# Second products of a feed-forward layer: 16 of 22 chunks of the sum by 2 x 2 blocks in three layers of four, with sums of weights made by adding transfers

## The chip, the cores and the metric

The kernel runs on one core of one Trainium2 chip. The metric is the device time of one execution in microseconds (us). Before the change the median of three runs is 2431.68 us (2431.58 to 2431.84).

## What is computed

Two layers of a transformer are applied to 512 rows of 1024 numbers, all in 32-bit floats. Each layer has a feed-forward network (FFN), a mix of three kinds of attention, and a second FFN, each with a residual sum and a layer norm. So there are four FFNs in a run. The part that the change touches is the product with `w2`:

```python
D_MODEL, SEQ, DEPTH, D_FF = 1024, 512, 2, 2816

def _swiglu(x, w1, w2):
    gt, up = jnp.split(x @ w1, 2, axis=-1)
    return (jax.nn.silu(gt) * up) @ w2

def reference(x, ...):
    for l in range(DEPTH):
        x = _layer_norm(DN_ALPHA * x + 0.5 * _swiglu(x, ffn1_w1[l], ffn1_w2[l]), ln1_g[l], ln1_b[l])
        mix = _token_mix(x, ...)
        x = _layer_norm(DN_ALPHA * x + mix, ln2_g[l], ln2_b[l])
        x = _layer_norm(DN_ALPHA * x + 0.5 * _swiglu(x, ffn2_w1[l], ffn2_w2[l]), ln3_g[l], ln3_b[l])
    return x
```

Here h = silu(gt) * up has 512 rows and 2816 columns, and `w2` has 2816 rows and 1024 columns.

## The kernel before

**Precision.** A 32-bit operand x is split into a high part (`hi`, ScalarE copies x to the matmul's format) and a rest (`lo`, VectorE subtracts the high part from x). A product of two operands is three matmuls: hi by hi, rest by hi, hi by rest. `wsplit` (lines 155 to 162) makes the two parts of a chunk of weights: one ScalarE instruction at line 160 and one VectorE instruction at line 161, 1024 elements in each partition.

**The second product.** The sum over 2816 runs in 22 chunks (`KF`) of 128. The result, 512 x 1024, lies in eight banks of PSUM, `accs[tb][hf]`: four blocks of rows by two halves of columns. A plain chunk costs 4 x 2 x 3 = 24 matmuls of 128x512 (`mm_rows`, line 195).

**Blocks.** `short_rows` (line 410) takes 12 chunks together as a 2 x 2 block product: the 512 rows in two halves, the 12 chunks in two halves of `NW` = 6, the 1024 columns in two halves. With seven products of blocks in place of eight (a Strassen-like scheme) it needs sums of parts of h and sums of blocks of weights first, and adds results into several quarters of the output afterwards. The quarters are `c11`, `c12`, `c21`, `c22`, two banks each; the blocks of h are `a11` to `a22`. One *step* of a product takes one pair of chunks of weights: `prod`, 2 banks x 2 chunks x 3 = 12 matmuls of 128x512 (line 453). Seven products of three steps are 21 steps. In the names that the change introduces the products are E, P, Z, S, T, R and F; in the code before they are `f_e`, `f_1`, `f_z`, `f_6`, `f_7`, `f_r` and `f_4`. E, P, S, T and F write into `c21`, Z into `c12`, R into `c11`. After E, P, S and T, `copies` takes `c21` to SBUF on ScalarE (line 459) and `add` adds the copy into another quarter on VectorE (line 464), which reads and writes that quarter's bank in PSUM.

**What runs around it.** Four plain chunks, 12 to 15 (`LEAD`), run ahead of the steps, while the first six transfers of weights into the tiles `b1` and `bt` land. Behind the steps follow chunk 16 and 17, plain, and then the last four, 18 to 21, in an order by rows, so that the layer norm can begin on the first 128 rows (`rows_ln`). The old input `xa` of the layer norm is loaded back from DRAM by POOL's queue into the space that `short_rows` leaves (line 622).

**Sums.** `a_parts` (lines 434 and 435) makes the two parts of a sum of h: one ScalarE and one VectorE instruction of 6 x 256 = 1536 elements in each partition. Sums of weights are VectorE instructions of 1024 elements (lines 490, 497, 517, 537): twelve in each FFN.

**Order.** TensorE and POOL run the program in the order in which it is written. For VectorE, ScalarE and the transfers of SP a scheduler sets the order when the program is built; each engine then runs its own list strictly in that order, and waits where an operand isn't there. `behind(...)` tells the scheduler to place instructions after a named one. In the first FFN, POOL also spreads 16 rows of a table (`after`, lines 441 to 444).

Of the kernel before, what the change touches and what calls it, by code (L numbers as in the profile page):

```python
# [66 lines left out]
def body(tc, a, out, depth=DEPTH):  # L67
# [87 lines left out]
    def wsplit(raw, n=KD, step=None):  # L155
        hi, lo = unit()
        step = step or n
        for i in range(0, n, step):
            c = slice(i, i + step)
            nc.scalar.activation(hi[:, c], raw[:, c], AF.Copy)  # L160
            nc.vector.tensor_tensor(lo[:, c], raw[:, c], hi[:, c].bitcast(F32), op=OP.subtract)  # L161
        return hi, lo
# [164 lines left out]
    NW = 6  # L327
    LEAD = range(2 * NW, KF - NTAIL - 2)
# [79 lines left out]
    def short_rows(st, w2, accs, hs, h_parts):  # L408

        V, A, tt = nc.vector, nc.scalar, nc.vector.tensor_tensor
        pl = pool("stp", side="right", reuse_waits="tile")
# [4 lines left out]
        sets.append(pl.tile([P, 2 * NW, 256], F32R, name="fs0"))
        pl.tile([P, S], F32, name="uc", tag="uc", bufs=4)
        bt = [pl.tile([P, KD, P], F32, name=f"bt{q}") for q in range(NW // 2)]  # L420
        sets.append(pl.tile([P, 2 * NW, 256], F32R, name="fs1"))
        c11, c12, c21, c22 = ([accs[i + t][j] for t in range(2)] for i in (0, 2) for j in range(2))
        a11, a12, a21, a22 = (st.ha[:, j:j + NW, i] for i in (H1, H2) for j in (0, NW))
        w = {}

        def rows(t, r, half, q):
            k0 = (r * NW + 2 * q) * P
            nc.sync.dma_start(t.rearrange("p (c k) f -> p c (k f)", c=2),
                              w2[k0:k0 + 2 * P, 512 * half:512 * half + 512].rearrange("(c p) f -> p c f", p=P))
            return t  # L430

        def a_parts(i, src):
            t = sets[i][:, 0:2 * NW]
            A.activation(t[:, 0:NW], src, AF.Copy)
            tt(t[:, NW:2 * NW], src, t[:, 0:NW].bitcast(F32), op=OP.subtract)
            return t
# [19 lines left out]
        def copies(o, n=None):  # L456
            d = n or [pl.tile([P, S], F32, name="uc", tag="uc", bufs=4) for _ in range(2)]
            for t in range(2):
                A.activation(d[t], o[t], AF.Copy)
            return d  # L460

        def add(o, x):
            for t in range(2):
                tt(o[t], o[t], x[t], op=OP.add)

        Q = range(NW // 2)

        for n, k in enumerate(LEAD):
# [3 lines left out]
            if n == 1:  # L472
                for q in Q:
                    rows(b1[q], 0, 0, q)
                    rows(bt[q], 0, 1, q)
                with behind(st.last):
                    tt(a21, a21, a22, op=OP.add)
                    f_e = a_parts(0, a21)
            if n == 2:
                with behind(st.last):  # L480
                    f_1 = a_parts(1, a11)
                    tt(a21, a21, a11, op=OP.subtract)
                    tt(a11, a12, a21, op=OP.subtract)
                    f_z = a_parts(2, a11)
            for tb in (2, 3, 0, 1) if n == len(LEAD) - 1 else range(NB):
                mm_rows(accs, lambda k: hs[k][:, 0], lambda k: hs[k][:, 1], k, tb, w, n == 0, False)
        copies(c21, xc)

        for q in Q:
            tt(bt[q], bt[q], b1[q], op=OP.subtract)  # L490
            prod(c21, f_e, b_parts(bt[q]), q, q == 0)
        copies(c21, ec)

        def z(q):
            r = rows(wraw(), 1, 1, q)
            prod(c12, f_z, b_parts(r), q)
            tt(bt[q], r, bt[q], op=OP.subtract)

# [1187 lines left out]
```

## Time and profile before

| what | value |
|---|---|
| median of three runs | 2431.68 us |
| the profiled execution | 2430.75 us |
| its span, first to last instruction | 2428.7 us |
| lead, chunks 12 to 15, second FFN | 1103.39 to 1125.18 us |
| steps, second FFN (252 matmuls) | 1125.18 to 1182.30 us |
| chunks 16 to 21, second FFN | 1182.30 to 1216.76 us |
| steps of the other three FFNs | from 261.62, 1465.72 and 2329.24 us |
| weight load (PEld) busy over the span | 2178.8 us (90%) |
| bytes moved by DMA | 286.29 MB, 118 GB/s on average |

Times inside the run count from the span's start. Of a group of instructions the profile gives the busy time and the mean duration in ns; instructions of one engine overlap by a little, so the distance from one start to the next is shorter than the duration. An "idle before" names what ended an engine's wait. The sums below are made for the second FFN, at 1103 to 1217 us; the third and the fourth have the same instructions.

### The profile page before, as it was taken

To read this page: it belongs to the slowest core of one execution; us is meant where nothing else is said; L and a number is where in the kernel's file an instruction comes from. 1 tells how busy PE (TensorE), PEld (TensorE's weight loads), DVE (VectorE), ACT (ScalarE), POOL (GpSimd) and SP (SyncE) were. 2 spreads that over 40 slices of the span, in tenths; PEclk is the share of its full clock that TensorE was granted. 3 is DMA by queue.
4 is the path that set the end of the run, shared out by engine and by line. 5 is a ranking of instruction groups with operands and counts; after the bars stand their busy time and mean duration, and the time that the engine had idled before them with its cause. 6 is when DMAs were issued, how large, how long until landed. Compare 5 with 4: busy or idle time off the path is not lost.

```text
span 2428.7 us, 42375 instructions
## 1 busy us (share of the span) xinstructions
PE 2417.4 (100%) x16257; PEld 2178.8 (90%) x16257; DVE 1945.4 (80%) x3786; ACT 1235.0 (51%) x2273; POOL 264.4 (11%) x472
## 2 busy tenths in 40 slices
PE   9999999999999999999999999999999999999998
PEld 9999888888889899998899998878888898999986
DVE  7997975687688689988789979666777886899795
ACT  4454544577644435445445445355766444445452
POOL 2000511133300000000000000122332000000000
PEclk9999999999999999999999999999999999999999
DMA  6332563533134433332533332645321344333233
GB/s 203 106 110 86 162 210 119 158 92 88 45 104 131 134 104 110 113 105 104 165 108 115 109 124 85 189 138 140 100 76 57 101 139 145 91 105 111 90 115 128
DMA packets 382699, 286.29 MB, mean 118 GB/s; under 512 B 17512, under 2 KB 347640, under 8 KB 382496
## 3 DMA queue, kind: packets, MB, share of 16 engines
q1 hardware_dynamic: 375024, 258.68, 35.9%
q0 software_dynamic: 7472, 24.90, 3.0%
q8 instruction: 128, 2.10, 0.4%
q14 instruction: 75, 0.61, 0.1%
HBM read 256.22 MB, written 17.88 MB: 113 GB/s over the span
## 4 chain that ended last, share of the span: by engine, by line
PE 99%; DMA 0%; DVE 0%; POOL 0%; SPq 0%; issue 0%; POOLq 0%; ACT 0%; DVEq 0%
PE pg L373 22%; PE acc L195 13%; PE pu L373 11%; PE acc L453 9%; PE pj L181 6%; PE pj L183 6%; PE pj L182 6%; PE pv L373 5%; PE brp L182 2%; PE brp L181 2%; PE brp L183 2%; PE sN L1081 2%; PE ptN L1123 1%; PE po L1142 1%; PE po L1029 1%; PE sF L1002 1%
## 5 line engine op out<-in xcount | busy, mean ns | idle before, releaser
L161 DVE TENSOR_TENSOR lo<-raw,hi 128x1024 fp32r<-128x1024 f32 x280 | 342.2, 1225 | 121.6 <-ACT hi L160 121.3
L160 ACT ACTIVATE hi<-raw 128x1024 fp32r<-128x1024 f32 x280 | 294.5, 1055 | 228.5 <-PE pg L373 56.9
L373 PE MATMUL pg<-xh,lo 128*128 128x256 f32 x1104 | 312.4, 283 | 0.0
L373 PE MATMUL pg<-xl,hi 128*128 128x256 f32 x1104 | 312.4, 283 | 0.0
L373 PE MATMUL pg<-xh,hi 128*128 128x256 f32 x1104 | 312.3, 283 | 0.0
L181 PE MATMUL pj<-xh,hi 128*128 128x512 f32 (+1 forms) x720 | 267.2, 371 | 0.5 <-ACT hi L1512 0.5
L355 ACT ACTIVATE hi<-ws 128x1024 fp32r<-128x1024 f32 x184 | 191.6, 1055 | 128.3 <-DVE ws L351 63.3
L183 PE MATMUL pj<-xh,lo 128*128 128x512 f32 (+1 forms) x720 | 254.6, 354 | 0.0
L182 PE MATMUL pj<-xl,hi 128*128 128x512 f32 (+1 forms) x720 | 254.4, 353 | 0.0
L356 DVE TENSOR_TENSOR lo<-ws,hi 128x1024 fp32r<-128x1024 f32 x184 | 223.4, 1221 | 38.3 <-ACT hi L355 37.5
L373 PEld LDWEIGHTS pg<-xh,hi 128*128 128x128 f32 x1104 | 211.9, 192 | 0.8
L373 PEld LDWEIGHTS pg<-xl,hi 128*128 128x128 f32 x1104 | 211.9, 192 | 0.8
L373 PEld LDWEIGHTS pg<-xh,lo 128*128 128x128 f32 x1104 | 211.9, 192 | 0.0
L373 PE MATMUL pu<-th,hi 128*128 128x256 f32 x608 | 172.1, 283 | 0.0
L373 PE MATMUL pu<-tl,hi 128*128 128x256 f32 x608 | 172.1, 283 | 0.0
L373 PE MATMUL pu<-th,lo 128*128 128x256 f32 x608 | 172.1, 283 | 0.0
L195 PE MATMUL acc<-hi,hs 128*128 128x512 f32 x512 | 158.2, 390 | 0.0
L183 PEld LDWEIGHTS pj<-xh,lo 128*128 128x128 f32 x720 | 136.1, 189 | 19.9 <-DVE lo L1513 0.2
L181 PEld LDWEIGHTS pj<-xh,hi 128*128 128x128 f32 x720 | 136.4, 189 | 15.5 <-issue 3.1
L358 ACT ACTIVATE dh<-raw 128x512 fp32r<-128x512 f32 x92 | 58.0, 631 | 177.5 <-PE pv L373 116.6
L182 PEld LDWEIGHTS pj<-xl,hi 128*128 128x128 f32 x720 | 136.8, 190 | 11.5 <-DVE xl L1598 0.2
L373 PEld LDWEIGHTS pu<-th,hi 128*128 128x128 f32 x608 | 116.7, 192 | 0.0
(394 smaller groups left out, 6501.5 us busy)
## 6 DMA issues: line engine op xcount, KB each, us to landing
raw<-in_ffn_w_dram SPq DMA_DIRECT2D x240, 512.0 KB, 3.8
raw<-in_w_in_dram SPq DMA_DIRECT2D x56, 512.0 KB, 3.8
raw<-in_w_gate_dram SPq DMA_DIRECT2D x48, 512.0 KB, 3.8
x_sp<-xa POOLq DMA_DIRECT2D x24, 512.0 KB, 5.8
ks<-hl SPq DMA_DIRECT2D x96, 128.0 KB, 2.3
xa<-x_sp POOLq DMA_DIRECT2D x16, 512.0 KB, 7.0
raw<-in_w_out_dram SPq DMA_DIRECT2D x16, 512.0 KB, 3.6
b<-in_ffn_w_dram SPq DMA_DIRECT2D x12, 512.0 KB, 7.6
```

What stands on the lines that cost most here:

```text
L160: nc.scalar.activation(hi[:, c], raw[:, c], AF.Copy)
L161: nc.vector.tensor_tensor(lo[:, c], raw[:, c], hi[:, c].bitcast(F32), op=OP.subtract)
L181: nc.tensor.matmul(o, hi[:, k], vh, start=first, stop=False)
L182: nc.tensor.matmul(o, hi[:, k], vl, start=False, stop=False)
L183: nc.tensor.matmul(o, lo[:, k], vh, start=False, stop=last)
L195: nc.tensor.matmul(o, x(k)[:, t], y[:, c], start=first and i == 0, stop=last and i == 2, skip_group_check=True)
L355: pa = nc.scalar.activation(hi, x, AF.Copy)
L356: pv = tt(lo, x, hi.bitcast(F32), op=OP.subtract)
L358: nc.scalar.activation(ud[0], ru[:, h2], AF.Copy)
L373: nc.tensor.matmul(o, wx, vx, start=first and k == 0 and i == 0, stop=k == 3 and i == 2, skip_group_check=True)
L453: nc.tensor.matmul(o[t], u[:, k, s], v[:, c], start=first and j == 0 and i == 0, stop=False, skip_group_check=True)
L1081: nc.tensor.matmul(o[:, 0:nb].rearrange("p k b j -> p (k b j)"), q, kx[:, 2 * b0:2 * (b0 + nb)].rearrange("p a b -> p (a b)"), start=i == ...
```

## The change

There are now two plans. `SLIM` keeps 12 chunks by blocks and is used in the first FFN. `WIDE`, in the other three, takes 16 chunks by blocks (`NW` = 8, seven products of four steps, 28 steps), has two plain chunks ahead (16 and 17), and behind the steps only the last four. The order of the steps is a string: a letter for the product and a digit for the pair of chunks, `ce`, `cp`, `cs` and `ct` for the copies and sums after E, P, S and T.

In `WIDE`, sums of weights are made by transfers that add: POOL issues them with `accum_op`, and the block of weights read from DRAM is added to what lies in the tile in SBUF. E's sums stay on VectorE (four of 1024 elements); S, T and F use tiles into which 4 + 4 + 4 transfers of 512 KB added, and four more plain transfers load `b1` anew for T. The parts of h rotate through three tiles instead of four; the sums and parts of h have 2048 elements. The parts of h for the chunks 19 to 21 are made ahead, at `ct`, in tiles (`tail`) that lie under `xa`.

```diff
     NTAIL = 4
-    NW = 6
-    LEAD = range(2 * NW, KF - NTAIL - 2)
+    WIDE = (8, range(16, 18), "R0 E0 E1 E2 E3 ce R1 P0 P1 P2 P3 cp R2 S0 R3 S1 Z0 S2 Z1 S3 cs Z2 T0 T1 T2 T3 ct Z3 F0 F1 F2 F3")
+    SLIM = (6, range(12, 16), "E0 E1 E2 ce Z0 P0 P1 P2 cp Z1 S0 Z2 S1 S2 cs R0 T0 T1 T2 ct R1 F0 R2 F1 F2")
...
+        NW, lead, order = plan
+        wide = plan is WIDE
...
+            tail = [st.late.tile([P, 2, S], F32R, name=f"hl{i}") for i in range(3)]
...
+        uc = 2 if wide else 4
...
+        sets = [x.rearrange("p a (b c) -> p (a b) c", b=2)[:, 0:2 * NW] for x in (xh, xl)]
+        names = ["fs0"] if wide else ["fs0", "fs1"]
...
+        def rows(t, r, half, q, add=False):
+            t_ = t.rearrange("p (c k) f -> p c (k f)", c=2)
+            if add:
+                nc.gpsimd.dma_start(t_, src(r, half, q), accum_op=OP.add)
+            else:
+                nc.sync.dma_start(t_, src(r, half, q))
             return t
...
+        def early():
+            if wide:
+                raws["R", 0] = rows(wraw(), 1, 0, 0)
+            for q in Q:
+                rows(b1[q], 0, 0, q)
+                rows(bt[q], 0, 1, q)
+        def parts_h(x):
+            if x == "E":
+                tt(a21, a21, a22, op=OP.subtract)
+                f["E"] = a_parts(0, a21)
+            if x == "P":
+                with behind(*mark):
+                    f["P"] = a_parts(1, a11)
+                    tt(a21, a21, a11, op=OP.subtract)
+                    tt(a11, a12, a21, op=OP.add)
+            if x == "Z":
+                f["Z"] = a_parts(1 if wide else 2, a11)
+            if x == "S":
+                f["S"] = a_parts(0 if wide else 3, a21)
+                V.scalar_tensor_tensor(a21, a21, -1.0, a22, op0=OP.mult, op1=OP.subtract)
+            if x == "T":
+                f["T"] = a_parts(2 if wide else 0, a21)
+            if x == "R":
+                f["R"] = a_parts(2 if wide else 1, a12)
+            if x == "F":
+                f["F"] = a_parts(0 if wide else 3, a22)
...
+                early()
+            if n == len(lead) - 1:
+                with behind(*st.last):
+                    for x in "RE" if wide else "EP":
+                        parts_h(x)
...
+        for op_ in order.split():
+            x = op_[0]
+            if x == "c":
+                y = op_[1]
+                u = copies(c21, ec if y == "e" else None)
+                if y == "e":
+                    add(c22, ec)
+                if y == "p":
+                    add(c11, u)
+                    for i in Q if wide else ():
+                        rows(b1[i], 1, 1, i, True)
+                if y == "s":
+                    for t in range(2):
+                        mark = lnq.copy, tt(u[t], ec[t], u[t], op=OP.subtract).ins
+                    add(c12, u)
+                if y == "t":
+                    add(c21, xc)
+                    add(c22, u, OP.subtract)
+                    with behind(*(mark if wide else ())):
+                        for i in range(3 if wide else 0):
+                            h_parts(KF - 3 + i, tail[i])
+                        h_parts(lead[-1] + 1, st.lnp.tile([P, 2, S], F32R, name="hs", tag="t2"))
+                continue
+            q = int(op_[1])
+            if x not in f:
+                with behind(*st.last):
+                    parts_h(x)
+            if x == "E":
+                tt(bt[q], bt[q], b1[q], op=OP.add)
+                prod(c21, f[x], b_parts(bt[q]), q, q == 0)
+                if wide and q == 3:
+                    mark = lnq.hi, lnq.lo
+                if wide:
+                    rows(bt[q], 1, 1, q, True)
+            if x == "P":
+                prod(c21, f[x], b_parts(b1[q]), q, q == 0)
+                if wide:
+                    b1[q] = rows(pl.tile([P, KD, P], F32, name=f"b1{q}", tag=f"b1{q}"), 0, 1, q)
+            if x == "Z":
+                r = rows(wraw(), 1, 1, q)
+                prod(c12, f[x], b_parts(r), q)
+                if not wide:
+                    tt(bt[q], bt[q], r, op=OP.add)
+            if x == "S":
+                prod(c21, f[x], b_parts(bt[q]), q)
+                if not wide:
+                    tt(b1[q], bt[q], b1[q], op=OP.subtract)
+            if x == "T":
+                if wide and q == 0:
+                    for i in Q:
+                        rows(bt[i], 1, 0, i, True)
+                prod(c21, f[x], b_parts(b1[q]), q)
+            if x == "R":
+                r = raws.get((x, q)) or rows(wraw(), 1, 0, q)
+                raws[x, q] = r
+                prod(c11, f[x], b_parts(r), q)
+            if x == "F":
+                if not wide:
+                    tt(bt[q], bt[q], raws["R", q], op=OP.add)
+                prod(c21, f[x], b_parts(bt[q]), q)
...
+        plan = SLIM if after else WIDE
...
+        short_rows(st, w2, accs, hs, h_parts, plan)
+        xap, xa = alloc_xa(st.late if plan is WIDE else None)
```

What the scheduler made of it, at three places of the second FFN. Names are those of the program with their numbers: `acc_12338` and `acc_12340` are the two banks of `c11` in the changed program, `acc_12339` and `acc_12341` those of `c12`, `acc_12342` and `acc_12344` of `c21`.

First, TensorE in the changed program at the end of P (weights `hi_12616` are step P3) and the start of R2 (`hi_12646`):

```order
L481 MATMUL acc_12344<-hi_12616,xl_90 128x512 x2
L481 MATMUL acc_12344<-lo_12617,xl_90 128x512
L481 MATMUL acc_12344<-hi_12616,xl_90 128x512 x2
L481 MATMUL acc_12344<-lo_12617,xl_90 128x512
L481 MATMUL acc_12338<-hi_12646,fs0_12416 128x512 x2
L481 MATMUL acc_12338<-lo_12647,fs0_12416 128x512
```

P3's last matmuls into `c21` are followed at once by R2 into `c11`. In the program before, where `c11` is `acc_12335` and `acc_12337`, `c12` is `acc_12336` and `acc_12338`, and `c21` is `acc_12339` and `acc_12341`, the end of P reads:

```order
L453 MATMUL acc_12341<-hi_12609,xl_90 128x512 x2
L453 MATMUL acc_12341<-lo_12610,xl_90 128x512
L453 MATMUL acc_12341<-hi_12609,xl_90 128x512 x2
L453 MATMUL acc_12341<-lo_12610,xl_90 128x512
L453 MATMUL acc_12336<-hi_12633,fs0_12354 128x512 x2
L453 MATMUL acc_12336<-lo_12634,fs0_12354 128x512
```

There a step of Z into `c12` stood behind P; now it is a step of R into `c11`, the quarter into which P's copy is added.

Second, VectorE in the changed program around that sum (L492 with `uc_12634` and `uc_12635` adds P's copy into the two banks of `c11`):

```order
L463 TENSOR_TENSOR xh_89<-ha_9936,xh_89 128x2048
L161 TENSOR_TENSOR lo_12647<-raw_12644,hi_12646 128x1024
L161 TENSOR_TENSOR lo_12666<-bt0_12366,hi_12665 128x1024
L161 TENSOR_TENSOR lo_12684<-raw_12681,hi_12683 128x1024
L161 TENSOR_TENSOR lo_12700<-bt1_12367,hi_12699 128x1024
L516 SCALAR_TENSOR_TENSOR ha_9936<-ha_9936 128x8x256
L492 TENSOR_TENSOR acc_12338<-acc_12338,uc_12634 128x512
L161 TENSOR_TENSOR lo_12720<-raw_12717,hi_12719 128x1024
L492 TENSOR_TENSOR acc_12340<-acc_12340,uc_12635 128x512
L463 TENSOR_TENSOR xl_90<-ha_9936,xl_90 128x2048
```

And the same place before, where the sum is L464 with `uc_12625` and `uc_12626`:

```order
L435 TENSOR_TENSOR xh_89<-ha_9933,xh_89 128x1536
L161 TENSOR_TENSOR lo_12656<-bt0_12356,hi_12655 128x1024
L517 TENSOR_TENSOR b11_12352<-bt1_12357,b11_12352 128x1024
L517 TENSOR_TENSOR b12_12353<-bt2_12358,b12_12353 128x1024
L161 TENSOR_TENSOR lo_12674<-raw_12671,hi_12673 128x1024
L161 TENSOR_TENSOR lo_12691<-bt1_12357,hi_12690 128x1024
L464 TENSOR_TENSOR acc_12335<-acc_12335,uc_12625 128x512
L161 TENSOR_TENSOR lo_12707<-bt2_12358,hi_12706 128x1024
L464 TENSOR_TENSOR acc_12337<-acc_12337,uc_12626 128x512
```

The sum stands behind four splits of weights and a 2048-element sum of h (L516) now, and behind splits and sums of weights before.

Third, VectorE in the changed program around the sum into `c12` at `cs` (L550 makes E minus S, L492 adds it, L620 are the parts of h for the last chunks):

```order
L161 TENSOR_TENSOR lo_12851<-b12_12614,hi_12850 128x1024
L550 TENSOR_TENSOR uc_12785<-ec0_12356,uc_12785 128x512
L492 TENSOR_TENSOR acc_12339<-acc_12339,uc_12785 128x512
L161 TENSOR_TENSOR lo_12867<-b13_12632,hi_12866 128x1024
L550 TENSOR_TENSOR uc_12786<-ec1_12357,uc_12786 128x512
L620 TENSOR_TENSOR hl0_12349<-hb_9935,hl0_12349 128x512
L620 TENSOR_TENSOR hl1_12350<-hb_9935,hl1_12350 128x512
L492 TENSOR_TENSOR acc_12341<-acc_12341,uc_12786 128x512
L620 TENSOR_TENSOR hl2_12351<-hb_9935,hl2_12351 128x512
L620 TENSOR_TENSOR hs_12896<-hb_9935,hs_12896 128x512
```

TensorE's next step behind `cs` is Z2, which writes `c12`. Between the sums into its two banks there stand a split of weights, the second difference and two parts of h; before, the step behind S's copy was one of R into `c11`, and no later step wrote `c12`.

More of the change, by code (lines that the diff above doesn't have):

```diff
@@ L299, in nx_close, with alloc_xa, release @@
         nx.pool = None
-    def alloc_xa():
+    def alloc_xa(under=None):
         p = pool("xap", side="right", reuse_waits="tile")
         xa = [p.tile([P, D], F32, name=f"xa{t}") for t in range(NB)]
-        p.tile([P, 88], F32, name="pad")
-        return p, xa
+        if not under:
+            p.tile([P, 88], F32, name="pad")
+        pools = K()
+        def release():
+            p.release()
+            if under:
+                under.release()
+        pools.release = release
+        return pools, xa
     halves = [slice(0, 256), slice(256, 512)]
@@ L456, in copies, with add @@
         def copies(o, n=None):
[L457 removed]
+            d = n or [pl.tile([P, S], F32, name="uc", tag="uc", bufs=uc) for _ in range(2)]
             for t in range(2):
[L459 removed]
+                lnq.copy = A.activation(d[t], o[t], AF.Copy).ins
             return d
[L462 removed]
+        def add(o, x, op=OP.add):
             for t in range(2):
[L464 to L468 removed]
+                tt(o[t], o[t], x[t], op=op)
+        f, raws, mark = {}, {}, ()
+        def early():
[24 more added lines that the diff above has]
+                f["F"] = a_parts(0 if wide else 3, a22)
+        for n, k in enumerate(lead):
             if k not in hs:
@@ L472, in short_rows @@
             if n == 1:
[L473 to L484, printed above, removed]
@@ L485, in short_rows @@
-            for tb in (2, 3, 0, 1) if n == len(LEAD) - 1 else range(NB):
+                early()
[3 more added lines that the diff above has]
+                        parts_h(x)
+            for tb in (2, 3, 0, 1) if n == len(lead) - 1 else range(NB):
                 mm_rows(accs, lambda k: hs[k][:, 0], lambda k: hs[k][:, 1], k, tb, w, n == 0, False)
         copies(c21, xc)
-        for q in Q:
-            tt(bt[q], bt[q], b1[q], op=OP.subtract)
-            prod(c21, f_e, b_parts(bt[q]), q, q == 0)
@@ L492, in short_rows @@
[L492 to L497, printed above, removed]
-        z(0)
-        f_6 = a_parts(3, a21)
-        for q in Q:
-            prod(c21, f_1, b_parts(b1[q]), q, q == 0)
-        u = copies(c21)
-        add(c22, ec)
-        z(1)
-        add(c11, u)
-        tt(a21, a22, a21, op=OP.subtract)
-        f_7 = a_parts(0, a21)
-        for q in Q:
-            prod(c21, f_6, b_parts(bt[q]), q)
-            if q == 0:
-                z(2)
@@ L513, in short_rows @@
-        u = copies(c21)
-        f_r = a_parts(1, a12)
-        f_4 = a_parts(3, a22)
-        for q in Q:
-            tt(b1[q], bt[q], b1[q], op=OP.subtract)
-        h_parts(LEAD[-1] + 1, st.lnp.tile([P, 2, S], F32R, name="hs", tag="t2"))
-        w = {}
-        def r_(q):
-            r = rows(wraw(), 1, 0, q)
-            w[q] = r
-            prod(c11, f_r, b_parts(r), q)
-        r_(0)
-        for t in range(2):
-            tt(u[t], u[t], ec[t], op=OP.add)
-        add(c12, u)
-        for q in Q:
-            prod(c21, f_7, b_parts(b1[q]), q)
@@ L541, in short_rows @@
+        if not wide:
+            pl.tile([P, 88], F32, name="pad")
         pl.release()
```

61 lines of the change are left out of this document (28 added, 33 removed).

## The prediction

> **What bounds the kernel now.** I read the page's busy times and its chain first, then the waits of TensorE alone.
>
> ```profile
> PE 2417.4 (100%) x16257; PEld 2178.8 (90%) x16257; DVE 1945.4 (80%) x3786; ACT 1235.0 (51%) x2273; POOL 264.4 (11%) x472
> PE 99%; DMA 0%; DVE 0%; POOL 0%; SPq 0%; issue 0%; POOLq 0%; ACT 0%; DVEq 0%
> PE warm L1494 <- DVE xl L1489: 1.1, 1, 1.1
> PE pj L181 <- ACT hi L1512: 0.5, 1, 0.5
> ```
>
> TensorE is the bound: it makes 99% of the chain, and its own waits (us in total, times, longest) are 1.6 us, all at the start. So a matmul taken away is worth its whole pace, and any wait put in front of TensorE costs its full length. What a matmul is worth stands in the chain of the second FFN (start, us, what):
>
> ```profile
> 1103.55 21.79 PE acc L195 x96
> 1125.34 57.12 PE acc L453 x252
> ```
>
> 57.12 / 252 = 0.2267 us for one 128x512, 2.72 us for a step of 12. The same stage by engine (PE, PEld, DVE, ACT, POOL busy, granted clock, DMA share, GB/s):
>
> ```profile
> 1103.39:1125.18 21.79, 21.79 (x99) 18.03 (x97) 21.29 (x19) 13.63 (x15) 0.00 (x0) 1.00 0.61 217
> 1125.18:1182.30 57.12, 57.12 (x254) 47.31 (x252) 52.61 (x50) 30.67 (x34) 0.54 (x1) 1.00 0.28 92
> ```
>
> VectorE is busy for 21.29 of the 21.79 us of the lead and 52.61 of the 57.12 us of the steps. It is the second bound here, and it has to run strictly in its own order. One pair of rows tells what that means: ScalarE copies P's result (`uc`), and VectorE adds it to `c11`.
>
> ```profile
> 1143.06 0.60 ACT L459 ACTIVATE uc<-acc 128x512 f32<-128x512 f32 x1 [0.53 <-PE acc L453]
> 1148.81 0.70 DVE L464 TENSOR_TENSOR acc<-acc,uc 128x512 f32<-128x512 f32 x1
> ```
>
> The copy ends at 1143.66, the sum starts at 1148.81: 5.15 us late, because four rows and the one that runs stand ahead of it. That costs nothing today, since TensorE's next steps write `c12` and `c21`. In the changed order its next step, R2, writes `c11`. This is the place that decides.
>
> **What the change removes.** A wide FFN has 2 + 4 plain chunks and 28 steps: 6 x 24 + 28 x 12 = 480 matmuls, where it had 10 x 24 + 21 x 12 = 492. Twelve fewer at 0.2267 us are 2.72 us for an FFN, 8.16 us for three. VectorE also loses twelve sums of 1024 and gains four; POOL gets twelve adding transfers.
>
> **What the change adds: the wait at R2.** I count VectorE's work from the split of R0 to the sum into `c11`, by its order in the changed program, with start-to-start distances of these rows:
>
> ```profile
> 1104.61 1.23 DVE L161 TENSOR_TENSOR lo<-raw,hi 128x1024 fp32r<-128x1024 f32 x1
> 1106.36 1.75 DVE L477 TENSOR_TENSOR ha<-ha 128x1536 f32<-128x1536 f32 x1
> 1108.03 1.75 DVE L435 TENSOR_TENSOR xl<-ha,xl 128x1536 fp32r<-128x1536 f32 x1
> 1136.86 1.22 DVE L161 TENSOR_TENSOR lo<-b,hi 128x1024 fp32r<-128x1024 f32 x1
> 1137.99 0.70 DVE L464 TENSOR_TENSOR acc<-acc,ec 128x512 f32<-128x512 f32 x1
> 1138.60 1.22 DVE L161 TENSOR_TENSOR lo<-raw,hi 128x1024 fp32r<-128x1024 f32 x1
> ```
>
> 1024 elements take 1.13 us (1136.86 to 1137.99), 512 take 0.61 us, 1536 take 1.67 us (1106.36 to 1108.03). So 512 more elements are 0.54 us, and 2048, which no row shows, are estimated at 2.20 us (bounds: 2.14 by three times the smallest step, 2.26 by two of 1024). The first split starts 1.22 us after the lead (1104.61 against 1103.39). From there to the sum stand 18 of 1024, 8 of 2048 and 3 of 512: 20.3 + 17.6 + 1.8 = 39.7 us, and 0.7 us for the sum itself: it ends 41.6 us after the lead's start if VectorE never waits. TensorE, by its order, comes to R2 after 2 x 24 + 10 x 12 = 168 matmuls: 38.1 us. That alone is a wait of 3.5 us.
>
> VectorE will wait, though, for weights. The lead is now two chunks, and nine transfers start with it where eight did.
>
> ```profile
> 1104.38 0.38 SPq L428 DMA_DIRECT2D raw<-in_ffn_w_dram  x1
> 1104.81 0.46 SPq L428 DMA_DIRECT2D b<-in_ffn_w_dram  x1
> raw<-in_ffn_w_dram SPq DMA_DIRECT2D x1, 512.0 KB, 3.8
> b<-in_ffn_w_dram SPq DMA_DIRECT2D x1, 512.0 KB, 5.5
> 1114.89 1.22 DVE L490 TENSOR_TENSOR bt<-bt,b 128x1024 f32<-128x1024 f32 x1 [0.50 <-DMA bt<-in_ffn_w_dram]
> 1112.00:1116.00 4.00, 4.00 (x19) 3.30 (x18) 3.50 (x3) 1.06 (x1) 0.00 (x0) 1.00 1.05 392
> ```
>
> The sequence begins as before: raw, b, bt, b, bt. The second bt ended VectorE's wait at 1114.89, 11.5 us after the lead's start. Behind it 512 KB at 392 GB/s take 1.34 us each, a pair 2.7 us: third bt at 14.2 us, fourth at 16.9. VectorE, undelayed, would reach the first bt 7.4 us after the lead's start; that bt landed between the b before it (1104.81 + 5.5 = 1110.3, so 6.9 us) and the second bt. With the fourth sum of weights starting at 16.9 us there remain to the sum 12 of 1024, 5 of 2048 and 2 of 512, then the sum: 13.6 + 11.0 + 1.2 + 0.7 = 26.5 us, so it ends at 43.4 us and R2 waits 5.3 us. Bounds: 3.5 without any wait for DMA, and 6.5 with the last four transfers at 320 GB/s in place of 392. I take 5.3, as the row above has such a wait for DMA already today. The second bank of `c11` follows behind one split: 0.61 + 1.13 + 0.70 - 0.70 after the first sum, against six matmuls (1.36): 0.4 us more.
>
> **The wait at Z2.** Behind `cs` TensorE goes straight to Z2, into `c12`. S's first bank is complete 1.2 us before Z2 could start (seven matmuls from the start of its last one, 1.59, less that one's 0.39); then the copy 0.60, the difference and the sum 0.70 each, and 0.1 of hand-overs: 2.1 - 1.2 = 0.9 us of wait. For the second bank VectorE does a split, the difference, two parts of h and the sum: 0.61 + 1.13 + 3 x 0.61 + 0.70 = 4.3 us from the first sum's start, while TensorE has 0.70 + 1.36 of that covered: 2.2 us. Before, nothing waited here, since no later step wrote `c12`. Bounds for both: 0.9 us, were the split and the parts of h not in between, and 3.7, with the third part of h ahead of the sum too.
>
> **Other parts.** E's and T's sums into `c22`, and T's into `c21`, have a step or more between; I take them at nothing. The parts of h for the last chunks move from behind the steps into them, which is the 2 x 0.61 just counted. The slim FFN has the same instructions in another order, at nothing. The adding transfers have no row; the nearest are POOL's plain loads:
>
> ```profile
> xa<-x_sp POOLq DMA_DIRECT2D x1, 512.0 KB, 3.5
> xa<-x_sp POOLq DMA_DIRECT2D x16, 512.0 KB, 7.0
> 1182.76 1.57 POOL L622 DMA_DIRECT2D xa<-x_sp  x3 [10.13 <-PE acc L453]
> ```
>
> One alone lands in 3.5 us, behind others in 7.0, and issuing takes 0.52 us. S0 comes some 20 us after its tile was free to be added to, T0 some 35, F0 some 30. So at 3.5 to 7 us each they cost nothing; I choose 0, and keep for the range that four in a row at 7 us or more would be late for S3 and T0. [...] `xa` queues behind these on POOL, and is needed only with the first layer norm, a lead's length later.
>
> **The clock.** A wait of 5 us may cost more than itself. At the end of this run TensorE goes idle, and at the start it comes from idle:
>
> ```profile
> 2418.77 0.39 PE L195 MATMUL acc<-lo,hs 128*128 128x512 f32 x1
> 2419.00:2421.50 2.50, 0.16 (x1) 0.00 (x0) 2.18 (x5) 1.24 (x4) 1.37 (x5) 1.00 0.46 169
> 2421.70:2428.70 7.00, 0.00 (x0) 0.00 (x0) 1.55 (x4) 0.00 (x0) 0.06 (x1) 0.50 0.21 75
> 1.11 3.78 PE L1494 MATMUL warm<-xl 128*128 128x128 f32 x16 [1.11 <-DVE xl L1489]
> 5.92 1.06 PE L1494 MATMUL warm<-xl 128*128 128x128 f32 x8
> ```
>
> The last matmul ends at 2419.16, and some 2.4 us later the granted clock is 0.50. At the start 16 matmuls take 3.78 us (0.24 each), and soon after 8 take 1.06 (0.13). So a wait of 5.3 us is long enough to halve the clock, and coming back takes up to 3.8 us at half pace, a loss of 0 to 1.9 us for each wait; I take 1.5, near the upper end that the start shows. [...]
>
> **The sum.** One wide FFN: -2.72 + 5.3 + 0.4 + 0.9 + 2.2 = +6.1 us; three: +18.2 us; three losses of clock: +4.5 us. From the profiled execution's 2430.75 us (span 2428.7 and 2.05 around it): 2453.5. The median of the runs is 0.93 us above that execution: **2454 us**, 0.9% slower.
>
> **Rivals.**
> *The clock stays full* (the wait turns out nearer 3.5 than 5.3, or falls badly for a drop): 2431.7 + 18.2 = 2450. For it: no drop inside a run is in the trace. Against it: 2.4 us sufficed at the end.
> *Adding transfers are the wait.* Place: S and T, where TensorE wants a tile that POOL's queue has not filled. Price: each four in a row at 10 us in place of 7 would be late by some 5 to 10 us in each wide FFN, so 2470 to 2490. For it: no row shows such a transfer, and the queue is one. Against it: 20 us and more of room.
> *VectorE keeps up: faster.* Place: the sum into `c11` ahead of R2. If 38.1 us suffice for VectorE's list (its rows shorter by 8%, or the sum's slot free of the 2048 rows), and the sums at `cs` hide in the same way, only the 8.2 us are left: 2423.5. For it: VectorE has eight sums of weights fewer, and its total over the FFN falls. Against it: the list up to the sum is counted, row by row, and that VectorE runs without a gap here is in the rows above. It decides from a list of 38.1 us downwards.
> *Only Z2 waits*: 3 x (3.1 - 2.72) = +1.1, so 2433, no change.
>
> **How the numbers follow.** Forecast 0.50, full clock 0.22, adding transfers 0.10, about half the waits (2442) 0.05, only Z2 0.05, faster 0.08. 0.2%, or 5 us, is about what a measurement of this kernel can tell from no change. Faster by more: 0.08; within: 0.05 and a little of the half, 0.06; slower: 0.86. The range reaches down to the full clock and half of the waits, 2440, and up to the low end of the slow transfers, 2472; outside lie the faster case, the Z2 case and most of the third.
>
> **What would show it.** TensorE's waits: "PE acc <- DVE acc" of some 5 us at R2 and 3 us at Z2, three times each. A granted clock under 1.00 just behind R2. VectorE without a gap from the lead to the sum into `c11`. Twelve matmuls fewer for an FFN. POOL's adding transfers landing in 3 to 7 us. I am wrong if TensorE shows no wait at R2 (VectorE kept up), or if its waits end at a DMA, or if the waits are there and the clock stays at 1.00.

## The result and the profile after

The changed kernel takes **2458.72 us** (median of four runs, 2456.44 to 2461.00), the kernel before 2431.63 us beside it: a ratio of 1.0112, 95% interval 1.0094 to 1.0129. It is 1.1% slower, 27 us. The forecast was 2454 us with a range of 2440 to 2472. The profiled execution took 2456.44 us, span 2454.7.

First the same two views as before: the page's busy times, and the waits of TensorE (us in total, times, longest).

```profile
PE 2420.8 (99%) x16221; PEld 2177.2 (89%) x16221; DVE 1942.3 (79%) x3759; ACT 1246.1 (51%) x2270; POOL 309.6 (13%) x508
```

```profile
PE acc L481 <- DVE acc L492: 21.4, 6, 5.2
PE acc L481 <- ACT hi L160: 2.7, 3, 0.9
```

36 matmuls fewer (16257 to 16221), as the change means them: 3 x 12. And 24.1 us of waits in the second products, where TensorE waited for nothing before. TensorE's busy time rose all the same, by 3.4 us, though 36 matmuls fewer should take 8.2 us off it. So matmuls became longer, which the next view explains. It cuts the place behind P in the second FFN into stretches of 3.41 us, as long as the shortest half clock inside this run (1496.98 to 1500.39, below). Each row gives the stretch and its length, the busy time of PE, PEld, DVE, ACT and POOL (with the number of instructions), the granted clock of TensorE (1.00 is full, 0.50 half), the DMA share and GB/s.

```profile
1142.00:1145.41 3.41, 0.42 (x2) 0.00 (x0) 3.41 (x4) 3.18 (x3) 0.05 (x1) 1.00 1.12 214
1145.41:1148.82 3.41, 1.20 (x3) 1.00 (x4) 3.41 (x4) 0.16 (x1) 3.41 (x3) 0.50 1.07 250
1148.82:1152.24 3.42, 3.42 (x10) 2.65 (x9) 2.67 (x2) 0.00 (x0) 0.18 (x1) 0.50 1.09 259
1152.24:1155.65 3.41, 3.41 (x17) 2.80 (x16) 1.23 (x1) 1.40 (x2) 0.46 (x1) 1.00 1.11 263
```

Read the first column behind the length and the clock together. TensorE is nearly idle in the first stretch; the clock is 0.50 in the next two; and the third, busy throughout, holds 10 matmuls where the fourth holds 17. All stretches at half clock inside this run, apart from its start and its end:

```profile
1145.41:1152.24 6.83, 4.62 (x11) 3.65 (x12) 6.08 (x5) 0.16 (x1) 3.59 (x3) 0.50 1.08 255
1496.98:1500.39 3.41, 3.22 (x8) 2.55 (x9) 3.41 (x4) 0.00 (x0) 0.00 (x0) 0.50 1.10 259
2367.38:2374.21 6.83, 5.81 (x14) 4.54 (x15) 4.89 (x5) 0.71 (x1) 0.39 (x1) 0.50 1.10 261
2398.10:2401.51 3.41, 3.41 (x10) 2.63 (x9) 3.39 (x4) 1.36 (x2) 0.00 (x0) 0.50 0.00 0
```

The first three follow the three waits at R2; the last one follows Z2 in the fourth FFN. TensorE is busy for 4.62 + 3.22 + 5.81 + 3.41 = 17.1 us in them, at 0.427 us from start to start (six matmuls from 1148.64 to 1151.20) in place of 0.2267. Half of that taken as lost is 8.5 us, an estimate (by the two paces it is 8.0).

Now the list of VectorE that the prediction counted, in the order of time (start, us). The lead of the second FFN starts at 1104.02.

```profile
1112.35 1.23 DVE L565 TENSOR_TENSOR bt<-bt,b 128x1024 f32<-128x1024 f32 x1 [0.87 <-DMA bt<-in_ffn_w_dram]
...
1120.82 1.23 DVE L565 TENSOR_TENSOR bt<-bt,b 128x1024 f32<-128x1024 f32 x1 [0.35 <-DMA bt<-in_ffn_w_dram]
...
1143.54 1.22 DVE L161 TENSOR_TENSOR lo<-bt,hi 128x1024 fp32r<-128x1024 f32 x1
1144.68 2.28 DVE L516 SCALAR_TENSOR_TENSOR ha<-ha 128x2048 f32<-128x2048 f32 x1
1146.88 0.69 DVE L492 TENSOR_TENSOR acc<-acc,uc 128x512 f32<-128x512 f32 x1
```

```profile
1147.62 1.22 PE L481 MATMUL acc<-hi,fs 128*128 128x512 f32 x2 [5.20 <-DVE acc L492]
```

The fourth sum of weights waits for its transfer and starts 16.8 us after the lead's start; the sum into `c11` ends at 1147.57, 43.55 us after it; R2 starts 0.05 us later, after 5.20 us of idle time. Last, Z2's place in the same FFN, all engines but the weight loads, with the rows that matter:

```profile
1171.87 0.70 DVE L492 TENSOR_TENSOR acc<-acc,uc 128x512 f32<-128x512 f32 x1
1172.60 0.58 ACT L487 ACTIVATE uc<-acc 128x512 f32<-128x512 f32 x1
1172.72 0.47 PE L481 MATMUL acc<-hi,xl 128*128 128x512 f32 x1 [0.89 <-ACT hi L160]
```

```profile
1174.47 1.29 DVE L620 TENSOR_TENSOR hl<-hb,hl 128x512 fp32r<-128x512 f32 x2
1175.67 0.69 DVE L492 TENSOR_TENSOR acc<-acc,uc 128x512 f32<-128x512 f32 x1
```

```profile
1176.42 0.74 PE L481 MATMUL acc<-hi,xl 128*128 128x512 f32 x2 [2.07 <-DVE acc L492]
```

Two parts of h (`hl`, 1.2 us from start to the sum's start) stand on VectorE right ahead of the second sum into `c12`, and TensorE waits for that sum. The first wait is put down to a split of weights on ScalarE that ends at 1172.69, while the first sum into `c12` ends at 1172.57. Experiment 9 tells the two apart: in its third FFN the split ends at 1507.18, the sum at 1507.85, and Z2 starts at 1508.00, 0.15 us behind the sum, as it does here. So the sum into `c12` held Z2 there, and the same distance speaks for it here.

### The profile page after: what moved, and what is told of

The parts are those of the page before. It is cut to its first block, busy times and chain, and to the rows that moved or that the text cites. A ratio compares the mean times of both kernels' runs of the same rounds, so it can differ in the third digit from the quotient of the medians.

```text
span 2454.7 us, 42385 instructions
## 1 busy us (share of the span) xinstructions
PE 2420.8 (99%) x16221; PEld 2177.2 (89%) x16221; DVE 1942.3 (79%) x3759; ACT 1246.1 (51%) x2270; POOL 309.6 (13%) x508
## 5 line engine op out<-in xcount | busy, mean ns | idle before, releaser
L161 DVE TENSOR_TENSOR lo<-raw,hi 128x1024 fp32r<-128x1024 f32 x274 | 334.7, 1225 | 116.7 <-ACT hi L160 115.7
L160 ACT ACTIVATE hi<-raw 128x1024 fp32r<-128x1024 f32 x274 | 288.0, 1055 | 213.3 <-PE pg L382 52.1
L455 POOL DMA_DIRECT2D bt<-in_ffn_w_dram x24 | 30.5, 1363 | 752.3 <-DVE lo L161 746.6
```

The lines of the kernel that those rows point to most:

```text
L160: lnq.hi = nc.scalar.activation(hi[:, c], raw[:, c], AF.Copy).ins
L161: lnq.lo = nc.vector.tensor_tensor(lo[:, c], raw[:, c], hi[:, c].bitcast(F32), op=OP.subtract).ins
L455: nc.gpsimd.dma_start(t_, src(r, half, q), accum_op=OP.add)
```

## The experiments

The kernel before ran beside each group, at medians of 2431.02, 2431.13 and 2431.22 us. Times are medians, ratios against the kernel before with a 95% interval.

**1. Other steps behind both copies.**

```diff
-... P3 cp R2 S0 R3 S1 Z0 S2 Z1 S3 cs Z2 T0 T1 T2 T3 ct ...
+... P3 cp S0 S1 R2 S2 Z0 R3 Z1 S3 cs T0 T1 Z2 T2 T3 ct ...
```

> The wide order with other steps put behind the two copies: behind P's copy S0 and S1 (into c21) stand ahead of R2, and behind S's copy T0 and T1 ahead of Z2. All matmuls, sums and transfers stay. Theory (TensorE's next step wanted the quarter that VectorE was still adding to): both waits and the half clock go, and what is left is the twelve matmuls fewer in three layers: 2431.6 - 3 x 2.72 = 2423.5 us, with up to 1 us for small hand-overs (2423 to 2426), and no wait of TensorE behind VectorE over 1 us in the second products. Rival (VectorE's whole list or the adding transfers are too slow, wherever the step stands): the waits turn up ahead of another step, 3 x 3 us or more, 2433 us and above.

Measured: **2423.71 us** (2423.28 to 2423.88), ratio 0.9969 (0.9957 to 0.9981), within the theory's range. TensorE's only wait in the wide second products that the view of waits lists is this one, and the steps of the second FFN run at clock 1.00:

```profile
PE acc L481 <- DVE lo L161: 0.2, 1, 0.2
```

```profile
1114.53:1191.67 77.14, 77.04 (x338) 62.78 (x336) 67.46 (x59) 46.50 (x48) 16.68 (x16) 1.00 0.93 246
```

Same matmuls, same VectorE instructions, same transfers: 35 us less than the changed kernel by the order of steps alone. VectorE is 67.46 us busy in 77.14, so it has room; it only needs the room at the right place. The rival, that VectorE or the transfers are too slow as a whole, falls. This version beats both kernels. That it comes so near to 2423.5 is in part chance. The steps of its three wide FFNs take 77.14, 77.33 and 77.25 us, some 1 us more each than 336 x 0.2267 = 76.17, in gaps of 0.1 to 0.3 us between matmuls. Against that, the run ends 7.4 us behind its last matmul, in this version as in the changed kernel, where it ended 9.5 us behind it before. Why it does was not tried.

**2. and 3. Each place alone.** In the second experiment only the order behind P's copy is changed, in the third only that behind S's (the two lines with a + are the second and the third).

```diff
-... cp R2 S0 R3 S1 Z0 S2 Z1 S3 cs Z2 T0 T1 T2 T3 ct ...
+... cp S0 S1 R2 R3 Z0 S2 Z1 S3 cs Z2 T0 T1 T2 T3 ct ...
+... cp R2 S0 R3 S1 Z0 S2 Z1 S3 cs T0 T1 Z2 T2 T3 ct ...
```

> Only the place behind P's copy is changed (S0 and S1 ahead of R2); Z2 still stands right behind S's copy. Theory: the 5 us at R2 go with their half clock, the waits of 0.89 and 2.07 us at Z2 stay: 2423.5 + 3 x 2.96 = 2432.4 us, and 0 to 3 us more if the clock falls to half behind some of them (2432 to 2436). Rival (VectorE is behind as a whole, and the wait at R2 only let it catch up): without the wait at R2 the wait at Z2 grows by up to 5 us, 2440 us or more.

> Only the place behind S's copy is changed (T0 and T1 ahead of Z2); R2 still stands right behind P's copy. Theory: waits of 5.20, 5.10 and 4.85 us at R2 stay, each with 3.4 to 6.8 us of half clock behind it (1.7 to 3.4 us lost): 2423.5 + 15.2 + 5 to 10 = 2444 to 2449 us. Rival (a wait costs its own length only, the half clock in the records costs nothing): 2438.7 us.

Measured: the third 2445.71 us (2444.48 to 2446.10), ratio 1.0059 (1.0044 to 1.0074), within its expectation. Its three waits at R2 are 15.4 us:

```profile
PE acc L481 <- DVE acc L492: 15.4, 3, 5.4
```

The second took **2439.48 us** (2437.60 to 2444.35), ratio 1.0037 (1.0025 to 1.0049): above the theory's range, and near the rival's. But its waits did not grow, as the rival would have it:

```profile
PE acc L481 <- DVE acc L492: 5.0, 4, 1.8
PE acc L481 <- ACT hl L619: 3.9, 2, 2.0
```

8.9 us in all, as expected, none longer than 2.0 us, though shifted: 1.96 and 0.89 us in the second FFN in place of 0.89 and 2.07. The missing 7 us are the clock again. Its stretches behind Z2 in the second FFN, and in the fourth:

```profile
1164.07:1167.49 3.42, 1.46 (x7) 0.94 (x6) 3.39 (x5) 2.89 (x6) 0.00 (x0) 1.00 1.10 247
1167.49:1170.90 3.41, 2.52 (x7) 1.51 (x6) 3.41 (x6) 2.88 (x4) 0.00 (x0) 0.50 0.69 126
1170.90:1174.31 3.41, 3.41 (x9) 2.67 (x9) 3.12 (x4) 1.06 (x1) 0.00 (x0) 0.50 0.02 5
2375.81:2379.22 3.41, 1.90 (x10) 1.28 (x8) 3.38 (x5) 2.35 (x5) 0.00 (x0) 1.00 1.11 259
2379.22:2382.63 3.41, 1.59 (x7) 0.98 (x7) 3.41 (x6) 3.41 (x5) 0.00 (x0) 1.00 0.71 129
2382.63:2386.04 3.41, 3.41 (x15) 2.84 (x16) 3.41 (x4) 1.33 (x2) 0.00 (x0) 1.00 0.00 0
```

With 1.46 us busy in a stretch, one wait of 1.96 us, the clock is half in the next one; it stayed half after 2.52 us busy and came back after a stretch that was busy throughout (3.41 us). In the fourth FFN the waits are 1.51 and 1.82 us, each in a stretch of its own (1.90 and 1.59 us busy), and nothing happens. What counts in these rows is how much of one stretch a wait takes, and not its length alone. The changed kernel shows the same: Z2's second wait is 2.07 us long in its second FFN and 2.08 in its fourth. In the second FFN two stretches share it and the clock stays full; in the fourth it falls into one stretch, and the clock drops behind that one (2398.10 above):

```profile
1172.72:1176.13 3.41, 1.63 (x6) 1.01 (x6) 3.41 (x5) 3.41 (x6) 0.00 (x0) 1.00 0.00 0
1176.13:1179.54 3.41, 3.12 (x14) 2.58 (x15) 3.41 (x4) 1.99 (x2) 0.00 (x0) 1.00 0.02 5
2394.69:2398.10 3.41, 1.33 (x6) 0.78 (x5) 3.41 (x6) 3.41 (x5) 0.00 (x0) 1.00 0.00 0
```

The expectation had allowed 0 to 3 us for the clock; it was 7 by the median. In the profiled execution two stretches of 6.83 us at half clock, busy for 5.93 and 6.08 us, cost 6.0, again estimated as half of that.

**4. Adding transfers made plain.**

```diff
-                nc.gpsimd.dma_start(t_, src(r, half, q), accum_op=OP.add)
+                nc.gpsimd.dma_start(t_, src(r, half, q))
```

> The changed kernel with POOL's twelve adding transfers in each wide layer made plain ones of the same tiles and bytes read: the sums of weights for S, T and F are left out. Theory (adding transfers are hidden): the same time as the changed kernel, 2456 to 2461 us, with the same waits at R2 and Z2. Rival (the adding slows VectorE or the weights that it waits for, and so makes the wait at R2): the wait at R2 falls by 1 us or more and the time by 3 us or more, below 2453 us.

Measured: 2458.91 us (2457.43 to 2460.97), the changed kernel's time. The groups of DMA issues (KB each, median us from issue to landing) of the changed kernel, and then of this one:

```profile
bt<-in_ffn_w_dram POOLq DMA_DIRECT2D x24, 512.0 KB, 9.1
b<-in_ffn_w_dram POOLq DMA_DIRECT2D x12, 512.0 KB, 11.0
```

```profile
bt<-in_ffn_w_dram POOLq DMA_DIRECT2D x24, 512.0 KB, 4.8
b<-in_ffn_w_dram POOLq DMA_DIRECT2D x12, 512.0 KB, 6.5
```

In this kernel adding costs some 4.4 us from issue to landing, and all of it lies beside other work.

**5. TensorE kept busy through the wait.** This separates the clock from the wait: VectorE's list and the wait for it stay, only TensorE isn't idle.

```diff
-    pace = const.tile([P, 48], F32, name="pace")[:, 0:1]
+    zt = const.tile([P, 48], F32, name="pace")
+    pace = zt[:, 0:1]
+    zero = zt[:, 16:48]
+    nc.gpsimd.memset(zero, 0.0)
...
                 if y == "p":
                     add(c11, u)
+                    for _ in range(24 if wide else 0):
+                        nc.tensor.matmul(c22[0][0:32, 0:P], zero, f["R"][:, 0, 0:P].bitcast(F32), start=False, stop=False,
+                                         skip_group_check=True)
```

> The changed kernel, and behind each P in a wide layer 24 more products of 128 columns whose weights are zeros, into a part of c22, so that TensorE works through most of the wait of 5.1 us at R2. VectorE's list and the waits for it stay. Theory (the idle time at R2 lets the clock fall, and that is a cost of its own): no half clock behind R2, R2's start at the same time after the lead, and the time falls by what the three half stretches cost, 6 to 7 us: 2450 to 2453 us. Rival (the half clock stands only in the records, or the waits alone make the time): 2457 to 2461 us, as the changed kernel.

Measured: **2450.37 us** (2448.89 to 2451.18), ratio 1.0079 (1.0064 to 1.0094). The products of zeros (each leaves two records) fill the wait, R2 starts 43.7 us after the lead (at 1103.75 here), where it was 43.6 in the changed kernel, and the clock is 1.00 over the place:

```profile
1142.03 5.43 PE L550 MATMUL acc<-fs,pace 128*32 128x128 f32 x48
1147.45 0.73 PE L484 MATMUL acc<-hi,fs 128*128 128x512 f32 x2
```

```profile
1141.70:1149.80 8.10, 8.02 (x59) 6.73 (x58) 8.10 (x8) 3.34 (x3) 3.64 (x3) 1.00 1.11 239
```

Work that computes nothing, put into a wait, makes the kernel 8 us faster by the medians, and 5.6 us by the profiled executions (2450.83 against 2456.44). The half clock behind Z2 was left alone: one stretch of 3.41 us, from 1174.61 on, is at half here. So the half clock is a cost of its own, beside the wait.

**6. One VectorE instruction moved behind the sum.** TensorE's order is the changed kernel's; the sum of h for T (L516 there) is issued behind the sums into `c11` (`late` is the second of them; `add` returns its last instruction here).

```diff
             if x == "S":
                 f["S"] = a_parts(0 if wide else 3, a21)
-                V.scalar_tensor_tensor(a21, a21, -1.0, a22, op0=OP.mult, op1=OP.subtract)
+                if not wide:
+                    V.scalar_tensor_tensor(a21, a21, -1.0, a22, op0=OP.mult, op1=OP.subtract)
...
-                    add(c11, u)
+                    late = add(c11, u)
...
+                if wide and x == "T":
+                    with behind(late):
+                        V.scalar_tensor_tensor(a21, a21, -1.0, a22, op0=OP.mult, op1=OP.subtract)
```

> The changed kernel in TensorE's own order; only VectorE's sum of parts of h for T (2048 elements, 2.20 us), which stood ahead of the sum into c11, is placed behind it. Theory (the wait at R2 is the length of VectorE's list ahead of that sum): the wait at R2 falls from 5.1 to about 2.9 us, Z2's stay at 0.89 and 2.07: 2458.7 - 3 x 2.2 = 2452 us, and 0 to 3 us less if the clock comes back sooner (2449 to 2452). Rival (the wait is the way from TensorE over ScalarE's copy, or late weights): the wait at R2 stays at 5 us, and the time at 2457 to 2461 us.

Measured: 2448.26 us (2447.05 to 2450.72), ratio 1.0072 (1.0055 to 1.0088), a little below the theory's range. The same place of VectorE and TensorE:

```profile
1143.72 1.22 DVE L161 TENSOR_TENSOR lo<-bt,hi 128x1024 fp32r<-128x1024 f32 x1
1144.86 0.69 DVE L492 TENSOR_TENSOR acc<-acc,uc 128x512 f32<-128x512 f32 x1
```

```profile
1145.60 0.73 PE L481 MATMUL acc<-hi,fs 128*128 128x512 f32 x2 [3.21 <-DVE acc L492]
```

The wait is 3.21 us (2.95 and 2.73 in the other two FFNs): 2.0 to 2.15 less, the length of the instruction that was moved. So the wait is set by VectorE's list ahead of the sum. The list includes VectorE's own stops for the weights of the lead; no run here takes those away. By the profiled executions the kernel is 7.7 us faster (2448.76 against 2456.44). Its waits are 6.3 us shorter, and the half clock costs some 1.8 us less (6.8 against 8.5): no stretch behind R2 is at half in the second FFN, one of 3.41 us behind R2 in each of the others, and one of 3.41 us behind Z2 in the third and the fourth. The medians differ by 10.5 us, because two of the four runs of the changed kernel took 2461 us.

**7. The order of experiment 1 in all four FFNs.**

```diff
-        plan = SLIM if after else WIDE
+        plan = WIDE
```

> The order of steps of e1_both_orders, in all four layers (the first one takes 16 chunks by blocks too). Theory (with no wait a step saved is worth its pace everywhere): 2423.7 - 2.72 = 2421.0 us, with up to 1.5 us for small waits in the first layer (2421 to 2422.5). Rival (POOL's queue, which in the first layer also writes a table, brings the adding transfers late, or VectorE cannot follow there): waits of 3 us or more in the first layer, 2424 us and above.

Measured: 2423.57 us (2422.88 to 2423.94), no different from experiment 1. A miss of the theory, though not by the rival's waits: the longest in the first FFN is 0.3 us. Its 336 matmuls of steps take

```profile
251.15:329.39 78.24, 77.75 (x337) 1.00 1.03 285
```

which is 2.1 us more than 336 x 0.2267. Gaps of a tenth to half a microsecond between matmuls, counted from start to start, eat most of the 2.72 us that twelve matmuls save.

**8. One step between instead of two,** against the order of experiment 1.

```diff
-... cp S0 S1 R2 S2 Z0 R3 Z1 S3 cs ...
+... cp S0 R2 S1 R3 Z0 S2 Z1 S3 cs ...
```

> The order of e1_both_orders, but with one step (S0) instead of two between P's copy and R2. Theory: one step covers 2.72 of the 5.2 us, so R2 waits 2.2 to 2.5 us and its second bank up to 0.4: 2423.7 + 3 x 2.5 = 2431 us; and as waits of 1.96 and 0.89 us halved the clock for 6.83 us in two layers of e2_cp_only, one of 2.2 us does so too in one to three layers: 2433 to 2441 us. Rival (a single wait under 3 us leaves the clock alone): 2430 to 2432 us.

Measured: 2433.60 us (2433.13 to 2435.12), ratio 1.0011 (1.0002 to 1.0020). The waits at R2 are 2.27, 2.07 and 1.82 us. They are 2.9 to 3.0 us shorter than the changed kernel's: one step, 2.72 us, covers about its own length and leaves the rest. In the profiled execution one of the three brought the half clock, and it was not the longest. The 2.27 us lay across two stretches (2.61 and 1.81 us busy); the 2.07 us fell into one (1.41 us busy):

```profile
1487.22:1490.63 3.41, 1.41 (x6) 1.05 (x6) 3.41 (x4) 0.97 (x2) 1.79 (x2) 1.00 1.10 244
1490.63:1494.04 3.41, 3.41 (x9) 2.48 (x8) 3.41 (x3) 0.34 (x1) 0.00 (x0) 0.50 1.09 253
```

**9. The parts of h behind the sum at `cs`.** Experiment 2 with one more edit; `add` returns its last instruction here.

```diff
                 if y == "s":
                     for t in range(2):
                         mark = lnq.copy, tt(u[t], ec[t], u[t], op=OP.subtract).ins
-                    add(c12, u)
+                    mark = mark[0], add(c12, u)
```

> The order of e2_cp_only (Z2 right behind S's copy, nothing waits at R2); only the parts of h for the last chunks, of which one or two of 0.61 us stood on VectorE ahead of the second sum into c12, are placed behind that sum. Theory (the waits at Z2 are VectorE's list, and the clock falls to half only where TensorE is idle for more than about 1.9 us of a 3.41 us stretch, as all such stretches so far show): the waits at Z2 fall from 2.9 to 1.8 to 2.3 us in a layer, and the two half stretches of 6.83 us in e2_cp_only go, since too little idle time is left in one stretch: 2423.7 + 3 x 2.1 = 2430 us (2429 to 2431.5), some 9 us less than e2_cp_only for two or three instructions of 0.61 us moved in each layer. Rival (the clock falls behind any pair of waits): 2435 to 2438 us, with half stretches in two or three layers.

Measured: 2434.31 us, but spread from 2431.66 to 2436.68 over ten runs, ratio 1.0014 (1.0004 to 1.0023). Above the expected 2429 to 2431.5, and 5 us below experiment 2, not 9. In the profiled execution (2432.37 us) the waits at Z2 are 1.9, 2.4 and 2.9 us in the three FFNs, more than the 2.1 expected on average. Moving the parts of h shortened the second wait as meant: it is 1.02 us in the second FFN and 0.74 in the others, where the changed kernel has 2.07 to 2.08. The first wait, ahead of which nothing was moved, is 0.90, 1.68 and 2.16 us. No stretch is at half clock. The stretch that came closest to bringing it, and the one behind it:

```profile
2369.19:2372.60 3.41, 1.64 (x8) 1.02 (x6) 3.38 (x5) 2.56 (x4) 0.00 (x0) 1.00 1.10 270
2372.60:2376.01 3.41, 2.28 (x9) 1.61 (x10) 3.38 (x6) 3.41 (x5) 0.00 (x0) 1.00 0.74 135
```

The slower runs of the ten have a lower mean clock, 0.997 at 2436 us against 0.999 at 2432. That speaks for half stretches in those runs, which have no trace. If so, the edit makes the drop rarer and doesn't exclude it. The median lies between the theory and the rival (2435 to 2438).

## Why the prediction was right, step by step

| step | forecast | measured |
|---|---|---|
| twelve matmuls fewer, each wide FFN | -2.72 us | 36 fewer in all |
| fourth sum of weights starts, after the lead's start | 16.9 us | 16.8 us |
| sum into `c11` ends, after the lead's start | 43.4 us | 43.55 us |
| wait at R2 | 5.3 us | 5.20, 5.10, 4.85 us |
| second bank at R2 | 0.4 us | no wait listed; 0.24 us in experiments 5 and 6 |
| first and second wait at Z2 | 0.9, 2.2 us | 0.89, 2.07 to 2.08 us |
| clock, three FFNs | 4.5 us | 8.5 us, estimated from the profiled execution |
| adding transfers | 0, landing in 3.5 to 7 us | no difference (experiment 4), landing in 9.1 and 11.0 us |

**The mechanism was right.** TensorE's new next step writes the quarter that VectorE still has to add to, and VectorE comes to that sum only when its own list allows. Experiment 1 takes the place away and both waits go; experiment 6 shortens VectorE's list by one instruction and the wait shortens by that instruction; experiment 4 changes the transfers and nothing happens. Counting VectorE's instructions from the row at the lead's start gave the sum's end to 0.2 us over 43 us, because the list ran nearly without a gap but for the waits for weights, which the prediction had priced from the landing of the transfers. It had put them all at the fourth sum of weights; in the trace one of 0.87 us stands ahead of the first and one of 0.35 ahead of the fourth, and the fourth starts when forecast. The estimate of 2.20 us from start to start for 2048 elements holds too (1144.68 to 1146.88).

**The term that was mis-sized is the clock.** "I take 1.5, near the upper end that the start shows" held each loss to at most half of 3.8 us, and gave Z2 none. In the profiled execution the half clock behind R2's three waits cost 2.3, 1.6 and 2.9 us and that behind Z2's one cost 1.7, estimated as half the busy time of each half stretch. Where the wait reached on into the half stretch, by 2.21 us from 1145.41 on (1.20 us busy) and by 1.02 us from 2367.38 on (2.40 us busy), a second stretch at half followed; where only 0.19 us of it did, from 1496.98 on (3.22 us busy), none did. That is how 6.83 us arise here, and the start of the run, where no such wait follows, couldn't show it. The other runs of the changed kernel reach 2461 us at a mean clock of 0.993 against this one's 0.995, so they lose more.

All three waits at R2 brought the half clock, though a wait of 5.3 us holds a whole stretch of 3.41 in only (5.3 - 3.41) / 3.41 = 55% of its places: behind R2 in the second FFN the stretch that brought the drop was busy for 0.42 us; in the other two it was idle throughout. The end of the kernel before already showed a drop without a wholly idle stretch. The last stretch at full clock there was busy for 0.97 us, and its clock falls only 2.4 us behind the last matmul, less than one stretch:

```profile
2418.19:2421.60 3.41, 0.97 (x5) 0.47 (x3) 2.65 (x7) 1.56 (x4) 1.47 (x5) 1.00 0.42 156
2421.60:2425.01 3.41, 0.00 (x0) 0.00 (x0) 1.65 (x4) 0.00 (x0) 0.16 (x1) 0.50 0.44 154
```

**The second bank** was an estimate at full clock. With the half clock the six matmuls ahead of it take 2.73 us (1147.62 to 1150.35) in place of 1.36 (6 x 0.2267), and the 0.4 us disappear behind them. In experiments 5 and 6, with the clock full there, the first matmul into the second bank starts 0.47 us behind the one before it in place of 0.23.

**The sum** of the profiled execution: -8.2 for matmuls, +24.1 waits, +8.5 clock is +24.4, against 2456.44 - 2430.75 = +25.7 measured. That these are so close is in part chance, since two small terms that the prediction did not have partly cancel. The steps of the second FFN,

```profile
1114.93:1202.40 87.47, 79.31 (x337) 64.33 (x336) 68.49 (x59) 47.44 (x48) 16.65 (x16) 0.96 0.84 216
```

take 87.47 us, 0.8 more than 336 x 0.2267 + 8.16 of waits + 2.3 of clock. Some 0.5 of these belong to the three listed waits: a matmul is drawn 0.39 us long and the next one follows 0.23 us after its start, so the view counts a wait from 0.16 us too late. The rest are gaps of about 0.1 us. The steps of the three FFNs together are 3.0 us over such a sum. Against that, the run ends 7.4 us behind its last matmul, where it ended 9.5 us behind it before; why it does was not tried. With both, the sum is +24.4 + 3.0 - 2.1 = +25.3.

**The rivals.** "The clock stays full" is what experiment 5 made true for R2: 2450.37 us, where the prediction had put that case at 2450. One half stretch behind Z2 is left in it, so the agreement to 0.4 us is in part chance. "Adding transfers are the wait" falls with experiment 4, though they land later than the prediction thought, the slowest into `bt` after 18.7 us. The room decided, not the landing time: in the second FFN the first of them is issued at 1118.35 and VectorE splits its tile for S0 at 1141.27. "VectorE keeps up" needed a list of 38.1 us; TensorE came after 38.4, the list ended at 43.55. What that rival promised, 2423.5, experiment 1 got by another way: not a faster VectorE, but a later R2. "Only Z2 waits" falls with the three waits at R2.

## What to carry to other kernels

When two engines both write an accumulator, look at what the matmul engine does next after handing one over: count the other engine's in-order list up to its write, and put as much independent work between as that list is long; here two steps were enough, one was not. An average of 79% busy says nothing about that place. And price a wait of TensorE at its length and, by these runs, up to some 3 us more for the clock, even where it is only 2 us long (experiment 2: an estimated 6.0 us for two FFNs).

## What the runs showed of the hardware

**The clock also fell to half behind stretches that were partly busy** (0.42 to 1.46 us of 3.41). In the rows quoted here from the second products the half clock lasts 3.41 us or twice that. In the changed kernel it begins at 1145.41, 1496.98, 2367.38 and 2398.10 us, the last three 351.57, 1221.97 and 1252.69 us behind the first, which is 103, 358 and 367 times 3.4133 us. With that whole execution cut in these steps, the stretches at full clock with a half one behind them have 0.00, 0.00, 0.42, 1.33 and, behind the last product, 1.40 us of busy TensorE; those without have 1.62 us or more. In the rows quoted from all runs the clock fell behind stretches with 1.46 us or less, and behind none with 1.52 us or more. The two nearest cases are the first row quoted of experiment 2 and this one of experiment 4, with the stretch that followed it at full clock:

```profile
1173.66:1177.07 3.41, 1.52 (x6) 0.91 (x6) 3.41 (x5) 3.41 (x6) 0.00 (x0) 1.00 0.00 0
1177.07:1180.48 3.41, 3.22 (x14) 2.69 (x15) 3.41 (x4) 1.89 (x2) 0.00 (x0) 1.00 0.02 5
```

So one wait of 1.96 us (experiment 2, second FFN) was enough for a drop, and the nearest stretches with and without one were 43 and 45% busy (1.46 and 1.52 of 3.41 us). To come back the clock took more in these two rows. A half stretch with 2.67 us busy (experiment 3) was followed by another, and one with 3.10 us (experiment 4) was the last:

```profile
1492.28:1495.69 3.41, 2.67 (x6) 2.15 (x7) 3.41 (x5) 0.00 (x0) 0.13 (x1) 0.50 1.09 255
1497.93:1501.34 3.41, 3.10 (x7) 2.48 (x8) 3.41 (x4) 0.00 (x0) 0.00 (x0) 0.50 1.04 384
```

**The place of a stretch against a wait differs** from FFN to FFN (1.63 and 1.33 us busy at the same wait in experiment 2's section) and, it seems, from run to run, and with it the time: ten runs of experiment 9 spread over 5 us, six of experiment 1, whose longest listed wait there is 0.2 us, over 0.6 us. That the place of the stretches makes the whole of that spread was not shown, since only one run of each has a trace.

**An adding transfer** of 512 KB into SBUF landed in 9.1 to 11.0 us (medians of the two groups), the same transfer without adding in 4.8 and 6.5. Issuing it kept POOL for 1.21 us (median), and 0.72 without adding.
